# Splitting weight tiles in halves, one of them through the raw ring, and a layer norm's bias placed behind two weight splits

## The chip, the cores and the metric

The kernel runs on one core of a Trainium2 chip. The time is the device time of one execution in microseconds. The kernel before takes 867.73 us, the median of three runs (867.6 to 867.78).

## The reference

One decoder layer over 512 tokens of width 1024, in float32, with inputs and weights in float32:

```
h   = layer_norm(x)                                     # "ln in"
q_g, k_g, v_g, r_g, a, q_lat, kv_lat, gates = split(h @ w_in)
o   = gated_linear_attention(q_g, k_g, v_g, a)          # 4 heads, in chunks; then rms_norm
y_gla = (o * silu(r_g)) @ w_o_gla                       # the GLA output
q, k, v from rms_norm(q_lat) @ w_q_b, rms_norm(kv_lat) @ w_kv_b, with rope
y_mla = softmax_attention(q, k, v) @ w_o_mla            # 8 heads, causal
mix = (sigmoid(gates0) * y_gla + sigmoid(gates1) * y_mla) @ w_out
h   = layer_norm(alpha * h + mix)
out = layer_norm(alpha * h + relu(h @ w_ff1)**2 @ w_ff2)
```

Both kernels compute all of it, with the same products.

## The kernel before, in words

**Float32 by three products.** TensorE multiplies float32 numbers that are rounded to a shorter form (fp32r). Every operand is therefore split into a high part, which ScalarE rounds by a copy, and a low part, which VectorE computes as the rest. A product is three matmuls: high by high, low by high, high by low. For activations the names are h, sh, so, ogT, latT; for weights they are `whi`/`wlo` (or `xh`/`xl` for tiles that stay).

**The stream of weights.** All weight tiles are entries of one list, `stream`, in the order in which the program uses them. `fetch` loads an entry (128 partitions x 1024 float32, 512 KB, or smaller) into a raw buffer `wraw`, a ring of three; `pump` splits entries one or two ahead of use, by one ScalarE copy and one VectorE subtraction over the whole tile, into `whi` and `wlo`, rings of two. Buffers come free in the order of the rings: a raw buffer when its split is done, a `whi` buffer when TensorE has used it for the last time. An entry may have `"fine"` (split per k-row), `"gates"` (instructions behind which its split must stand) and a `"home"`: "r" puts its two parts in two `wraw` buffers instead.

**Seven products instead of eight.** Large products are done as Strassen-like units of seven products with sums of weight tiles and of activations: "11", "t1", "22", "t2", "t3", "21", "t4" (t marks a sum of weights, which lies in a buffer `wq`). The units in the middle of the kernel are `g0` and `g1` (the two halves of the gates) and `yg` (the GLA output). Each product has two column groups (0 and 1) with a weight tile of 4 k-rows x 256 columns each, and a tile serves 24 matmuls of 256 columns (L1299 to L1301).

**Order of use.** `lat` (the latents, two tiles of 2 x 360 columns at a time), q, k, v, r, then `g0` and `g1`, then `yg` 11, t1, 22, t2, then the first rope part of the queries (`qr`, L279 to L281), `yg` t3, then the pair 0 of heads: `qn`, `kn` (L279 to L281) and `mv` (the values, L313 to L315), then `yg` 21. `latT` are latent tiles loaded back from HBM (`latd`) for them, on SyncE's queue like the weights; they use the buffers in which raw weights and sums lay.

**The front.** The first two token tiles are normalised and transposed first, and the latents of these two are computed (`gemm_tm` with the first two `tts`) while `ln_in1` normalises the third and fourth (`x_112`, `x_114` in the rows): statistics (`bst`, `mvin`), the power on GpSimd, the bias `nmr` on VectorE, then the application on ScalarE. Their transposes (L505) follow on TensorE, and `h` on ScalarE from them. The splits of latent weight tiles lie between on ScalarE and VectorE; `issue_after` and `chain` say which instruction must stand behind which.

The order of an engine's instructions is set when the kernel is built: a scheduler arranges the instructions of the program within its dependencies, and an edit at one place can move rows at others. Each engine runs its row of instructions strictly in that order.

Of the kernel before, what the change touches and what calls it, by code (L numbers as in the profile page):

```python
# [19 lines left out]
P = 128  # L20
T = 512
D = 1024
NT = T // P
# [29 lines left out]
def tile_hybrid_block(ctx: ExitStack, tc: tile.TileContext, I, out, dbg=None):  # L53
    nc = tc.nc
# [49 lines left out]
    chain = {}  # L104
# [18 lines left out]
    mm = nc.tensor.matmul  # L123
# [17 lines left out]
    xt = []  # L141
# [12 lines left out]
    ident = ca[:, 0:P]  # L154
# [14 lines left out]
    stream = []  # L169
# [41 lines left out]
    def pump(i):  # L211
        fetch(i + 1 + DMA_AHEAD)
        while st["spl"] < min(len(stream), i + 2 + SPLIT_AHEAD):
            e = stream[st["spl"]]
            if st["spl"] > i + e.get("ahead", SPLIT_AHEAD) and not e["res"]:
                break
            nk, n = e["nk"], e["n"]
            hi, lo = [A([P, nk, T * 2 // nk], F32R, w) for w in HOME["a" if e["res"] else e.get("home", "w")]]
            raw = e["src"]() if "src" in e else e.pop("raw")
            with ExitStack() as gates:  # L220
                for g in e.get("gates") or st["gates"] or (st.get("pt", ()) if e.get("late") else ()):
                    gates.enter_context(tc.issue_after(g.ins))
                for k in [slice(i, i + 1) for i in range(nk)] if e.get("fine") else [slice(0, nk)]:
                    st["ins"] = act(hi[:, k, :n], raw[:, k, :n], AF.Copy)
                    st["lo"] = vtt(lo[:, k, :n], raw[:, k, :n], f(hi[:, k, :n]), op=ALU.subtract)
            st["gates"] = ()
            e["w"] = (hi, lo)
            if "post" in e:
                e["post"](raw)
            if "post2" in e:  # L230
                later[st["spl"] + 2] = lambda p=e["post2"], r=raw: p(r)
            later.pop(st["spl"], lambda: None)()
            st["spl"] += 1
# [57 lines left out]
        tick(width)  # L291
        return accs

    def gemm_tm(pls, xs, n, evac, width=None, tts=range(NT), guard=None, ks=None, accs=None, new=None, fine=False):
        accs = {} if accs is None else accs
        ticks = [0]
        share = n <= 256 and len(pls) == 1 and len(tts) == NT
        nk = pls[0]["nk"]
        for k in ks or range(nk):
            ws = [weights(pl, k) for pl in pls]  # L300
            first, last = k == 0, k == nk - 1
            for tt in tts:
                c = slice(tt * P, (tt + 1) * P)
                xh, xl = xs[k][:, 0, c], xs[k][:, 1, c]
                for j, (hi, lo) in enumerate(ws):
                    if first:
                        if share and tt % 2:
                            accs[tt, j] = accs[tt - 1, j][:, 256:]
                        else:
                            accs[tt, j] = (new or MM)()  # L310
                    o = accs[tt, j][:, :n]
                    opens = first and not (share and tt % 2)
                    mm(o, xh, hi[:, :n], start=opens, stop=False, skip_group_check=share)  # L313
                    mm(o, xh, lo[:, :n], start=False, stop=False, skip_group_check=share)  # L314
                    mm(o, xl, hi[:, :n], start=False, stop=last, skip_group_check=share)  # L315
                ticks[0] += 1
                if fine is True or fine and ticks[0] % fine == 0:
                    tick(width)
            if not last and not fine:
                tick(width)  # L320
        if evac is None:
            return accs
        if guard:
            guard()
        todo = [(tt, j) for tt in tts for j in range(len(pls))]
        for i, (tt, j) in enumerate(todo):
            evac(tt, j, accs[tt, j])
            if i == len(todo) // 2 - 1:
                pump(pls[-1]["idx"][-1] + 1)
        tick(width)  # L330
# [65 lines left out]
    def plan_unit(*seq):  # L396
        for key, op in seq:
            for g in range(UNITS[key][2]):
                PL[key, op, g] = len(stream)
                e = {"nk": 4, "n": 256, "res": False}  # L400
                if op[0] != "t" and (op, key) not in HELD:
                    e["dmas"] = [(slice(0, 4), u_src(key, int(op[0]) - 1, int(op[1]) - 1, g), None)]
                else:
                    e["src"] = lambda q=(key, (op, g)): WQ[q]
                    if key == "g0" and op in ("t1", "t2"):
                        e["ahead"], e["home"] = 2, "wr"[g]
                if op == ("t1" if key == "g0" else "22"):
                    e["post"] = lambda raw, q=(key, "t1", "t2", g): u_sum(*q, WQ[q[0], ("22", q[3])] if q[0] == "g0" else raw)
                    if key == "f1":
                        e["post2"] = lambda raw, q=(key, "12", "t3", g): u_sum(*q, raw)  # L410
                elif op == "21" and key == "yg":
                    e["post"] = lambda raw, g=g: u_sum("yg", "t2", "t4", g, raw)
                elif op == "t2" and key == "g1":
                    e["post"] = lambda raw, g=g: u_acc("g1", "t2", "t4", g, "21")
                elif op == "t2" and key != "yg":
                    e["post2" if key == "f1" else "post"] = lambda raw, q=(key, "t2", "t4", g): u_sum(*q, WQ[q[0], ("21", q[3])])
                stream.append(e)
# [53 lines left out]
        fb += nb  # L471


    def ln_rows(src, dst, mv, on_act=False, behind=None):
        bst = S([P, 2, 6], F32, "bst")
        for j in range(2):
            with ExitStack() as gates:
# [6 lines left out]
        if on_act is not False:  # L484
            nmr = S([P, 1], F32, "nmr")
            chain.pop("dve", None)
            behind = st["nmr"] = stt(nmr, mv[:, 0:1], -1.0, mv[:, 1:2], op0=ALU.mult, op1=ALU.mult)
            for j in range(2):
                c = slice(j * T, (j + 1) * T)
# [8 lines left out]
    def ln_transpose(rows, g, b, outs, hf, alt=False, n="h0"):  # L498
        tk = slice(hf * 256, (hf + 1) * 256)
        for k in range(NK):  # L500
# [1 line left out]
                outs.append(A([P, 2, T], F32R, n) if n == "h0" else (B([P, T], F32R, n), B([P, T], F32R, n)))  # L502
            p = MM() if alt and k in (4, 5) else PX()
            for i in range(2):
                nc.tensor.transpose(p[:, i * P:(i + 1) * P], rows[2 * hf + i][:, k * P:(k + 1) * P],  # L505
                                    identJ if hf and n == "h0" else ident)
            tmp = B([P, 256], F32, "lnt")
            hi, lo = part(outs[k], 0, tk), part(outs[k], 1, tk)
            ha = act(hi, p[:, :256], AF.Identity, scale=g[:, k:k + 1], bias=b[:, k:k + 1])
# [648 lines left out]
    def ln_in1():  # L1158
        for i in range(4):
            yield  # L1160
        for tt in (2, 3):
            chain.update(dve=st["lo"] if tt == 2 else st["nmr"])
            ln_rows(xt[tt], xt[tt], mvin[:, tt, :], on_act=((0, 1), (0,))[tt - 2])
            chain.clear()
            stream[tt + 3]["gates"] = (st["var"],)
            yield
            if tt == 2:
                yield
# [35 lines left out]
    for hf in range(2):  # L1204
# [6 lines left out]
            finish(t_ln1)  # L1211
            st["gates"] = st["h0"]
        for i in range(2):
            gemm_tm([PL["lat", i]], hT, half, ev_lat(i), tts=(2 * hf, 2 * hf + 1), guard=lat_guard if i and not hf else None)
    t_lat = spawn(latents())
    t_he = spawn(h_early())
    gemm_fm(PL["q"], hT, T, ev_q)
# [607 lines left out]
```

## Time and profile before

| | |
|---|---|
| median of three runs | 867.73 us |
| the profiled execution | 867.63 us |
| its span | 865.8 us |
| mean granted clock of TensorE | 0.998 |
| TensorE busy | 853.8 us, 99% |
| VectorE, ScalarE, GpSimd busy | 656.5, 491.9, 136.5 us |
| chain that ended last | TensorE 95%, VectorE 3%, ScalarE 1% |

A row of the timeline gives the start and duration in us from the span's start, the engine, the source line (L111 is the helper through which ScalarE and VectorE instructions are issued), the operation, the names out<-in, the shape, and how many such rows in a run are put together (x2). In square brackets stands how long the engine was idle before it, and what released it. Matmuls overlap: each lasts longer than the distance to the next one's start. A group row gives the count, the busy sum, the mean duration in ns, and the idle time ahead of them. A row by windows gives the window, its length, and for TensorE, its weight load, VectorE, ScalarE and GpSimd the busy us with the number of instructions, then granted clock, share of the DMA engines and GB/s.

### The profile page before, as it was taken

Reading aid. Unit: us, or ns where it says so; the run is one execution under the profiler, and the core shown is the slowest. Engines: PE = TensorE matmul, PEld = TensorE weight load, DVE = VectorE, ACT = ScalarE, POOL = GpSimd, SP = SyncE. Lnnn points to the kernel's source line nnn. Section 1 sums busy time; section 2 is a strip of 40 time slices with the busy share of each in tenths; the row PEclk is TensorE's granted clock in tenths of the full one; section 3 lists DMA queues with packets and bytes.
Section 4 is the critical chain, followed back from the end, with each engine's and each line's share of the span. In section 5 each row is a group of like instructions: output and inputs, shape, how many; then the busy total and the mean of one; then the engine's idle time right before and its main releaser. Section 6 shows DMA issues by size and latency. Waiting matters only on the chain.

```text
span 865.8 us, 13210 instructions
## 1 busy us (share of the span) xinstructions
PE 853.8 (99%) x4887; PEld 752.8 (87%) x4887; DVE 656.5 (76%) x1141; ACT 491.9 (57%) x863; POOL 136.5 (16%) x179
## 2 busy tenths in 40 slices
PE   8999999999999999999999999999999999999996
PEld 7988888889999998988888889988888888889985
DVE  7857889977578858897856878985567546888865
ACT  6556977655566754565745334475466446766820
POOL 1530001110221103030000021005301520141000
PEclk9999999999999999999999999999999999999999
DMA  9896946696649916233155355009922990499312
GB/s 317 226 199 175 345 148 167 212 264 209 148 148 238 205 43 171 56 104 98 32 176 217 120 167 190 1 1 267 256 61 51 304 214 16 104 243 232 106 69 75
DMA packets 101231, 137.94 MB, mean 159 GB/s; under 512 B 13201, under 2 KB 66116, under 8 KB 101168
## 3 DMA queue, kind: packets, MB, share of 16 engines
q1 hardware_dynamic: 76512, 91.35, 33.6%
q0 software_dynamic: 22784, 41.10, 22.7%
q10 hardware_dynamic: 1872, 4.66, 1.4%
q8 instruction: 38, 0.62, 0.3%
q14 instruction: 25, 0.20, 0.1%
HBM read 113.49 MB, written 8.91 MB: 141 GB/s over the span
## 4 chain that ended last, share of the span: by engine, by line
PE 95%; DVE 3%; ACT 1%; DMA 0%; issue 0%; POOL 0%; POOLq 0%; DVEq 0%
PE mm L279 10%; PE mm L280 10%; PE mm L281 10%; PE mm L1301 6%; PE mm L1299 6%; PE mm L1300 6%; PE mm L314 5%; PE mm L315 5%; PE mm L313 5%; PE px L1633 3%; PE px L1634 3%; PE px L1635 3%; PE mm L1633 2%; PE mm L1634 2%; PE mm L1635 2%; PE mm L863 1%
## 5 line engine op out<-in xcount | busy, mean ns | idle before, releaser
L111 DVE TENSOR_TENSOR wlo<-wraw,whi 128x1024 fp32r<-128x1024 f32 (+2 forms) x96 | 96.0, 1006 | 65.2 <-ACT whi L111 65.1
L111 ACT ACTIVATE whi<-wraw 128x1024 fp32r<-128x1024 f32 (+2 forms) x96 | 84.1, 884 | 77.2 <-PE mm L280 20.7
L111 DVE TENSOR_TENSOR wlo<-wq,whi 128x1024 fp32r<-128x1024 f32 x52 | 63.6, 1223 | 31.9 <-ACT whi L111 31.7
L280 PE MATMUL mm<-h,whi 128*128 128x512 f32 x224 | 87.2, 389 | 0.0
L279 PE MATMUL mm<-h,whi 128*128 128x512 f32 x224 | 87.1, 390 | 0.0
L281 PE MATMUL mm<-h,wlo 128*128 128x512 f32 x224 | 83.2, 390 | 0.0
L111 ACT ACTIVATE whi<-wq 128x1024 fp32r<-128x1024 f32 x52 | 55.0, 1058 | 33.6 <-PE mm L1300 16.1
L1652 POOL DMA_DIRECT2D res<-ev x42 | 38.4, 1064 | 180.7 <-ACT ev L111 150.0
L1301 PE MATMUL mm<-sh,wlo 128*128 128x256 f32 x176 | 50.0, 284 | 0.3 <-DVE wlo L111 0.2
L1299 PE MATMUL mm<-sh,whi 128*128 128x256 f32 x176 | 50.0, 284 | 0.0
L1300 PE MATMUL mm<-sh,whi 128*128 128x256 f32 x176 | 49.8, 283 | 0.0
L279 PEld LDWEIGHTS mm<-h,whi 128*128 128x128 f32 x224 | 42.1, 188 | 8.8
L281 PEld LDWEIGHTS mm<-h,wlo 128*128 128x128 f32 x224 | 42.0, 188 | 8.7
L280 PEld LDWEIGHTS mm<-h,whi 128*128 128x128 f32 x224 | 42.1, 188 | 8.6
L111 ACT ACTIVATE relu<-mm 128x512 f32<-128x512 f32 x26 | 15.2, 594 | 41.9 <-PE mm L281 41.9
L111 ACT ACTIVATE xh<-wraw 128x1024 fp32r<-128x1024 f32 (+1 forms) x24 | 24.1, 1014 | 26.1 <-PE mm L315 15.2
L111 DVE TENSOR_TENSOR xl<-wraw,xh 128x1024 fp32r<-128x1024 f32 (+1 forms) x24 | 27.9, 1171 | 11.8 <-ACT xh L111 11.8
L1301 PEld LDWEIGHTS mm<-sh,wlo 128*128 128x128 f32 x176 | 33.8, 192 | 0.7 <-DVE wlo L111 0.7
L1300 PEld LDWEIGHTS mm<-sh,whi 128*128 128x128 f32 x176 | 33.8, 192 | 0.0
L1299 PEld LDWEIGHTS mm<-sh,whi 128*128 128x128 f32 x176 | 33.8, 192 | 0.0
L1301 PE MATMUL mm<-h,wlo 128*128 128x256 f32 x112 | 32.1, 287 | 0.0
L1299 PE MATMUL mm<-h,whi 128*128 128x256 f32 x112 | 31.8, 284 | 0.0
(487 smaller groups left out, 2784.0 us busy)
## 6 DMA issues: line engine op xcount, KB each, us to landing
wraw<-in_w_ff_dram SPq DMA_DIRECT2D x36, 512.0 KB, 5.0
wraw<-in_w_in_dram SPq DMA_DIRECT2D x30, 512.0 KB, 5.1
wq<-in_w_ff_dram POOLq DMA_DIRECT2D x26, 512.0 KB, 9.4
res<-ev POOLq DMA_DIRECT2D x42, 256.0 KB, 9.9
wq<-in_w_in_dram POOLq DMA_DIRECT2D x20, 512.0 KB, 10.1
wq<-in_w_in_dram SPq DMA_DIRECT2D x18, 512.0 KB, 7.5
hsd<-hs SPq DMA_DIRECT2D x16, 256.0 KB, 3.9
xr<-hsd SPq DMA_DIRECT2D x16, 256.0 KB, 4.3
```

The source lines that it names most:

```text
L111: ins = op(*a, **k)
L279: mm(o, hi[:, c], xh, start=first, stop=False)
L280: mm(o, hi[:, c], xl, start=False, stop=False)
L281: mm(o, lo[:, c], xh, start=False, stop=last)
L313: mm(o, xh, hi[:, :n], start=opens, stop=False, skip_group_check=share)
L314: mm(o, xh, lo[:, :n], start=False, stop=False, skip_group_check=share)
L315: mm(o, xl, hi[:, :n], start=False, stop=last, skip_group_check=share)
L1299: mm(oa, hi[:, k, c], xh, start=opens and k == 0 and a == 0, stop=False, skip_group_check=True)
L1300: mm(oa, hi[:, k, c], xl, start=False, stop=False, skip_group_check=True)
L1301: mm(oa, lo[:, k, c], xh, start=False, stop=k == 3, skip_group_check=True)
L1633: mm(o, xh[:, c], hi[:, pp], start=opens, stop=False, skip_group_check=True)
L1634: mm(o, xh[:, c], lo[:, pp], start=False, stop=False, skip_group_check=True)
```

## The change

It has three parts.

1. Every weight tile of `g1` and `yg` gets `"cut": 2`: its split is done in two halves of two k-rows (128 x 512 each), high and low of the first half, then of the second.
2. Column group 1 of `yg` t3 gets the home "r": its two parts lie in two buffers of the raw ring instead of a `whi` and a `wlo` buffer.
3. In the front, while the third token tile is normalised, the splits of stream entries 5 and 6 are placed between its variance and its bias; before, entry 5 stood behind the third tile's variance and 6 behind the fourth's, and now 7 stands behind the fourth's. TensorE's matmuls of the last k-row of the second latent half are put behind the transpose number 1 of the new tokens (`held`, `st["tp"]`).

```diff
@@ pump
-                for k in [slice(i, i + 1) for i in range(nk)] if e.get("fine") else [slice(0, nk)]:
+                step = 1 if e.get("fine") else nk // e.get("cut", 1)
+                for k in [slice(i, i + step) for i in range(0, nk, step)]:
                     st["ins"] = act(hi[:, k, :n], raw[:, k, :n], AF.Copy)
                     st["lo"] = vtt(lo[:, k, :n], raw[:, k, :n], f(hi[:, k, :n]), op=ALU.subtract)
@@ gemm_tm(..., held=False)
-                    mm(o, xh, hi[:, :n], start=opens, stop=False, skip_group_check=share)
+                    with ExitStack() as gates:
+                        if last and held and tt == tts[0]:
+                            gates.enter_context(tc.issue_after(st["tp"].ins))
+                        mm(o, xh, hi[:, :n], start=opens, stop=False, skip_group_check=share)
@@ plan_unit
                 e = {"nk": 4, "n": 256, "res": False}
+                if key in ("g1","yg"):
+                    e["cut"] = 2
+                if (key, op, g) == ("yg", "t3", 1):
+                    e["home"] = "r"
@@ ln_rows(..., between=None)
             chain.pop("dve", None)
+            if between is not None:
+                between()
             behind = st["nmr"] = stt(nmr, mv[:, 0:1], -1.0, mv[:, 1:2], op0=ALU.mult, op1=ALU.mult)
@@ ln_transpose
-                nc.tensor.transpose(p[:, i * P:(i + 1) * P], rows[2 * hf + i][:, k * P:(k + 1) * P],
-                                    identJ if hf and n == "h0" else ident)
+                tp = nc.tensor.transpose(p[:, i * P:(i + 1) * P], rows[2 * hf + i][:, k * P:(k + 1) * P],
+                                         identJ if hf and n == "h0" else ident)
+            if n == "h0" and k == 1:
+                st["tp"] = tp
@@ ln_in1
+        def splits():
+            stream[5]["gates"] = (st["var"],)
+            pump(4)
+            chain.update(dve=st["lo"])
+
         for tt in (2, 3):
             chain.update(dve=st["lo"] if tt == 2 else st["nmr"])
-            ln_rows(xt[tt], xt[tt], mvin[:, tt, :], on_act=((0, 1), (0,))[tt - 2])
+            ln_rows(xt[tt], xt[tt], mvin[:, tt, :], on_act=((0, 1), (0,))[tt - 2], between=splits if tt == 2 else None)
             chain.clear()
-            stream[tt + 3]["gates"] = (st["var"],)
+            if tt == 3:
+                stream[7]["gates"] = (st["var"],)
@@ the latents' calls of gemm_tm
+                    held=i and not hf)
```

How the rows move at the places of which the prediction speaks. First VectorE in the front, before; `nmr_289` and `nmr_315` are the biases of the third and fourth token tile, `xl` low parts of latent weight tiles:

```order
L111 TENSOR_TENSOR xl_300<-wlo_233,xh_299 128x2x360
L111 SCALAR_TENSOR_TENSOR nmr_289<-mvin 128x1
L111 BN_STATS bst_309<-x_114 128x6 x2
L111 BN_AGGR mvin<-bst_309 128x2
L111 TENSOR_SCALAR mvin<-mvin 128x1
L111 TENSOR_TENSOR xl_328<-wlo_235,xh_327 128x2x360
L111 SCALAR_TENSOR_TENSOR nmr_315<-mvin 128x1
L111 TENSOR_SCALAR x_114<-x_114,mvin 128x512
L111 TENSOR_TENSOR xl_369<-wraw_237,xh_368 128x2x360
```

The same place now:

```order
L111 TENSOR_TENSOR xl_291<-wlo_233,xh_290 128x2x360
L111 TENSOR_TENSOR xl_295<-wlo_235,xh_294 128x2x360
L111 SCALAR_TENSOR_TENSOR nmr_289<-mvin 128x1
L111 BN_STATS bst_313<-x_114 128x6 x2
L111 BN_AGGR mvin<-bst_313 128x2
L111 TENSOR_SCALAR mvin<-mvin 128x1
L111 TENSOR_TENSOR xl_369<-wraw_237,xh_368 128x2x360
L111 SCALAR_TENSOR_TENSOR nmr_319<-mvin 128x1
L111 TENSOR_SCALAR x_114<-x_114,mvin 128x512
```

Both low parts stand ahead of the first bias now, and the third one ahead of the second bias. TensorE behind the fourth token tile's last early transpose, up to the first matmul on the new h (`h_16_140` with `mm_459`), before:

```order
L505 MATMUL px_378<-ca,x_114 128x128
L314 MATMUL mm_340<-xl_369,h_41_202 128x360
L315 MATMUL mm_340<-xh_368,h_41_202 128x360
L314 MATMUL mm_344<-xl_369,h_41_202 128x360
L315 MATMUL mm_344<-xh_368,h_41_202 128x360
L313 MATMUL mm_340<-xh_368,h_44_210 128x360
L314 MATMUL mm_340<-xl_369,h_44_210 128x360
L315 MATMUL mm_340<-xh_368,h_44_210 128x360
L313 MATMUL mm_344<-xh_368,h_44_210 128x360
L314 MATMUL mm_344<-xl_369,h_44_210 128x360
L315 MATMUL mm_344<-xh_368,h_44_210 128x360
L313 MATMUL mm_459<-xh_136,h_16_140 128x360
```

And now (the same source lines are five lines further down):

```order
L516 MATMUL px_378<-ca,x_114 128x128
L318 MATMUL mm_340<-xh_368,h_44_210 128x360
L319 MATMUL mm_340<-xl_369,h_44_210 128x360
L320 MATMUL mm_340<-xh_368,h_44_210 128x360
L318 MATMUL mm_459<-xh_136,h_16_140 128x360
```

Ten matmuls stood between, three are left; seven have moved ahead of the transposes. SyncE at `yg` t3, where it loads weights of qn (`w_q_b`), of kn (`w_kv_b`) and two latent tiles, before:

```order
L208 DMA wraw_3784<-in_w_q_b_dram 128x2x128
L208 DMA wraw_3857<-in_w_q_b_dram 128x2x128 x2
L208 DMA wraw_3895<-in_w_kv_b_dram 128x2x128 x2
L1414 DMA latT_3661<-latd_1180 128x1024
L1414 DMA latT_3663<-latd_1220 128x1024
```

And now:

```order
L208 DMA wraw_3830<-in_w_q_b_dram 128x2x128
L1435 DMA latT_3703<-latd_1180 128x1024
L1435 DMA latT_3705<-latd_1220 128x1024
L208 DMA wraw_3905<-in_w_q_b_dram 128x2x128 x2
L208 DMA wraw_3943<-in_w_kv_b_dram 128x2x128 x2
```

The loads of qn's second tile and of kn's tile have gone behind the latents; by the ring, the first takes the buffer of qn's first tile and the second that in which t3's high part lay. ScalarE at the same place, with the splits of qr's second tile (`whi_3758`) and of t3's groups 0 and 1 (`whi_3768`, `whi_3786`), before:

```order
L111 ACTIVATE whi_3758<-wraw_3701 128x2x256
L111 ACTIVATE u_688_3734<-mm_3500 128x512
L111 ACTIVATE tabw_3741<-cs 128x512
L111 ACTIVATE tabw_3749<-sn 128x512
L111 ACTIVATE tab_3739<-px_3740 128x512
L111 ACTIVATE whi_3768<-wq_3377 128x1024
L111 ACTIVATE whi_3786<-wq_3380 128x1024
```

And now:

```order
L111 ACTIVATE wraw_3832<-wq_3406 128x512 x2
L111 ACTIVATE whi_3802<-wraw_3745 128x2x256
L111 ACTIVATE u_688_3778<-mm_3532 128x512
L111 ACTIVATE tabw_3785<-cs 128x512
L111 ACTIVATE tabw_3793<-sn 128x512
L111 ACTIVATE tab_3783<-px_3784 128x512
L111 ACTIVATE whi_3812<-wq_3403 128x512 x2
```

Group 1 (`wraw_3832`) has moved from the last place to the first, ahead of qr's second tile; each split counts two rows now.

More of the change, by code (lines that the diff above doesn't have):

```diff
@@ L292, in gemm_fm, with gemm_tm @@
         return accs
[L294 removed]
+    def gemm_tm(pls, xs, n, evac, width=None, tts=range(NT), guard=None, ks=None, accs=None, new=None, fine=False,
+                held=False):
         accs = {} if accs is None else accs
@@ L471, in tile_hybrid_block, with ln_rows @@
         fb += nb
-    def ln_rows(src, dst, mv, on_act=False, behind=None):
+    def ln_rows(src, dst, mv, on_act=False, behind=None, between=None):
         bst = S([P, 2, 6], F32, "bst")
@@ L1213, in tile_hybrid_block @@
         for i in range(2):
-            gemm_tm([PL["lat", i]], hT, half, ev_lat(i), tts=(2 * hf, 2 * hf + 1), guard=lat_guard if i and not hf else None)
+            gemm_tm([PL["lat", i]], hT, half, ev_lat(i), tts=(2 * hf, 2 * hf + 1), guard=lat_guard if i and not hf else None,
+                    held=i and not hf)
     t_lat = spawn(latents())
```

## The prediction

> **What bounds the kernel now.** I read the page's totals and chain first, then the waits of TensorE (us in total, times, longest), of which four belong to places that the change touches.
>
> ```profile
> span 865.8 us, 13210 instructions
> ...
> PE 95%; DVE 3%; ACT 1%; DMA 0%; issue 0%; POOL 0%; POOLq 0%; DVEq 0%
> ...
> PE mm L314 <- DVE xl L111: 0.4, 1, 0.4
> PE mm L314 <- DVE wlo L111: 0.2, 1, 0.2
> PE mm L1299 <- ACT whi L111: 0.2, 1, 0.2
> PE mm L1301 <- DVE wlo L111: 0.2, 1, 0.2
> ```
>
> TensorE is the bound: 95% of the chain, and the change leaves its 4718 rows of work as many as they are. So the time can only move by TensorE's idle moments, and the waits listed make 1.0 us. They understate a stall: matmuls overlap, and their ends are modelled. I therefore read starts against the usual spacing, in TensorE's timeline (start, us, instruction):
>
> ```profile
> 23.80 0.60 PE L505 MATMUL px<-ca,x 128*128 128x128 f32 x4
> 24.78 0.43 PE L314 MATMUL mm<-xl,h 128*128 128x360 f32 x1 [0.38 <-DVE xl L111]
> ...
> 28.75 0.32 PE L315 MATMUL mm<-xh,h 128*128 128x360 f32 x1
> 28.91 0.32 PE L313 MATMUL mm<-xh,h 128*128 128x360 f32 x1
> ...
> 275.78 0.28 PE L1299 MATMUL mm<-sh,whi 128*128 128x256 f32 x1
> 275.90 0.28 PE L1300 MATMUL mm<-sh,whi 128*128 128x256 f32 x1
> 276.33 0.39 PE L1301 MATMUL mm<-sh,wlo 128*128 128x256 f32 x1 [0.15 <-DVE wlo L111]
> 276.55 0.28 PE L1299 MATMUL mm<-sh,whi 128*128 128x256 f32 x1
> ...
> 279.19 0.28 PE L1300 MATMUL mm<-sh,whi 128*128 128x256 f32 x1
> 279.60 0.39 PE L1301 MATMUL mm<-sh,wlo 128*128 128x256 f32 x1
> ...
> 296.85 0.28 PE L1300 MATMUL mm<-ogT,whi 128*128 128x256 f32 x1
> 297.13 0.39 PE L1301 MATMUL mm<-ogT,wlo 128*128 128x256 f32 x1
> ...
> 325.63 0.28 PE L1300 MATMUL mm<-ogT,whi 128*128 128x256 f32 x1
> 326.15 0.39 PE L1299 MATMUL mm<-ogT,whi 128*128 128x256 f32 x1 [0.24 <-ACT whi L111]
> ...
> 332.23 0.39 PE L281 MATMUL mm<-latT,wlo 128*128 128x512 f32 x1
> 332.58 0.50 PE L279 MATMUL mm<-latT,whi 128*128 128x512 f32 x1
> ...
> 338.83 0.40 PE L313 MATMUL mm<-whi,latT 128*128 128x256 f32 x2
> 339.47 0.39 PE L314 MATMUL mm<-wlo,latT 128*128 128x256 f32 x1 [0.25 <-DVE wlo L111]
> ```
>
> A 256-wide matmul starts 0.12 us after the last (275.78, 275.90), a 360-wide one 0.16, a 512-wide one 0.23 (the 332 rows' usual step). After a stall the next step is longer too: 276.33 to 276.55 is 0.22, so each stall has 0.1 us of refill behind it. That gives what each costs: at 24 us four transposes end near 24.1 and the next matmul starts at 24.78, 0.6 + 0.1 = 0.7; at 276, 0.43 - 0.12 + 0.1 = 0.4; at 279, 0.4; at 297, 0.28 - 0.12 + 0.1 = 0.25; at 326, 0.52 - 0.12 + 0.1 = 0.5; at 332.6, 0.35 - 0.23 + 0.1 = 0.2; at 339, 0.64 - 0.24 + 0.1 = 0.5. **The sum, 2.95 us, is the ceiling of what the change can win.**
>
> **Part one, halves (second gate unit and GLA output).** It adds instructions and moves no arithmetic. Groups by shape (busy us, mean ns of one), the low parts concerned, and VectorE's load in its fullest stretch (after the sum, mean busy columns PE, PEld, DVE, ACT, POOL):
>
> ```profile
> L111 DVE TENSOR_TENSOR wlo<-wraw,whi 128x1024 fp32r<-128x1024 f32 x60 | 73.5, 1224 | 52.5 <-ACT whi L111 52.4
> L111 DVE TENSOR_TENSOR wlo<-wraw,whi 128x512 fp32r<-128x512 f32 x30 | 20.0, 686 | 11.3 <-ACT whi L111 11.3
> L111 ACT ACTIVATE whi<-wraw 128x1024 fp32r<-128x1024 f32 x60 | 63.5, 1058 | 42.6 <-PE mm L280 14.8 <-PE mm L1300 7.4 <-DMA wraw<-in_w_ff_dram 6.7
> L111 ACT ACTIVATE whi<-wraw 128x512 fp32r<-128x512 f32 x30 | 18.1, 628 | 25.4 <-issue 12.5 <-PE mm L280 5.3 <-PE mm L1300 5.1
> ...
> 275.05 1.22 DVE L111 TENSOR_TENSOR wlo<-wraw,whi 128x1024 fp32r<-128x1024 f32 x1
> 278.33 1.22 DVE L111 TENSOR_TENSOR wlo<-wq,whi 128x1024 fp32r<-128x1024 f32 x1
> ...
> 280.00:300.00 20.00, 20.00 (x167) 19.80 (x167) 18.74 (x32) 15.36 (x30) 3.69 (x3) 1.00 0.95 216
> ```
>
> A tile's first low half is there 1.22 - 0.69 = 0.53 us earlier than the whole, and where ScalarE leads, another 1.06 - 0.63 = 0.43. At 276 the half ends at 275.05 + 0.69 = 275.74, before the 276.02 at which TensorE wants it: 0.4 saved. At 279 it ends at 279.02 against 279.31 wanted, but TensorE comes 0.4 earlier by then, and VectorE's queue is what is late: 0.15 to 0.4 saved. At 297, 0 to 0.25 for the same reason. I take **-0.85**, bounds -0.4 (only the first) and -1.05.
>
> The price: 28 tiles (two units, seven products, two column groups) get one more instruction on each of two engines, at most 2 x 0.686 - 1.224 = 0.15 us on VectorE and 2 x 0.628 - 1.058 = 0.2 on ScalarE. Back to back they overlap, the lower end is near 0. Seven such tiles lie in 280 to 300, so VectorE goes from 18.74 to at most 19.8 of 20: still covered by TensorE's work, without slack. If that cover is gone, each further 0.1 on VectorE is 0.1 of time.
>
> [...]
>
> **Part two, the GLA output's third sum in the raw ring.** The sum's high and low part take two turns of a ring of three, so, as SyncE's rows in the change's section show, qn's second tile and kn's tile are now loaded behind two latent tiles. On ScalarE the sum's split of group 1 comes forward ahead of qr's second tile. It no longer needs a whi buffer that TensorE frees, so 326's 0.5 goes; and mv's low part now stands ahead of gate products on VectorE, so 339's 0.5 can go. SyncE's and ScalarE's rows of before, with median us to landing:
>
> ```profile
> 321.49 0.88 SPq L208 DMA_DIRECT2D wraw<-in_w_kv_b_dram  x2
> 326.02 1.70 SPq L1414 DMA_DIRECT2D latT<-latd  x2
> ...
> wraw<-in_w_kv_b_dram SPq DMA_DIRECT2D x16, 128.0 KB, 2.3
> latT<-latd SPq DMA_DIRECT2D x5, 512.0 KB, 4.1
> latd<-latT SPq DMA_DIRECT2D x5, 512.0 KB, 6.0
> ```
>
> The row at 326.02 is released by the low part of the sum's group 0, whose place on VectorE hardly moves. So the latents still go out at 326.0 to 327.7, then qn's two loads to 328.6. Alone they land by 328.15 + 2.3 = 330.5; behind the second latent, whose 4.1 runs from 326.9 to 331.0, somewhat later: 330.5 to 331.5, split 0.63 later, 331.1 to 332.1. TensorE wants them at 332.35 - 0.5 = 331.85. That is between 0.2 won (332.6's stall) and 0.25 lost. Kn's load now waits for the sum's last matmul, near 331.2, and its second piece lands at 331.2 + 0.45 + 2.3 = 334.0; split 334.6, low part 335.3, wanted 334.6 (twelve 512-wide steps after 331.85) and 335.1: 0 to 0.3 lost. Before, that load went out at 321.49. Queued behind it on SyncE are mv's load and the 512 KB of the GLA output's next product; mv's is not wanted before 337.4, so they have 2 us to spare. Part two: **-0.7**, between -1.2 and, if 339's wait stays and both loads are late, 0.05 lost.
>
> **Part three, the front.** On VectorE the bias (nmr) of the third token tile now follows two low parts (xl) of weights instead of one:
>
> ```profile
> 20.75 0.91 DVE L111 TENSOR_TENSOR xl<-wlo,xh 128x720 fp32r<-128x720 f32 x1
> 22.11 0.16 DVE L111 SCALAR_TENSOR_TENSOR nmr<-mvin 128x1 f32<-128x1 f32 x1 [0.44 <-POOL mvin L483]
> 23.82 0.91 DVE L111 TENSOR_TENSOR xl<-wlo,xh 128x720 fp32r<-128x720 f32 x1
> 27.18 1.93 ACT L111 ACTIVATE h<-px,ca 128x256 fp32r<-128x256 f32 x4
> ```
>
> The second low part moves from 23.82 to 20.75 + 0.9 = 21.6 and is done at 22.5, long before 24.1: 0.7 goes. What is late next is the bias, 22.11 to 22.5, and with it the third tile's normalisation on ScalarE (behind it there: the fourth tile's, a weight split and the quarters of h) and the fourth tile's statistics, each by 0.4. The gate on `st["tp"]` and the later bias also change TensorE's order: the third tile's transposes move behind the first matmuls of the last weight tile, seven more matmuls (0.16 each) precede the fourth tile's, and three instead of ten stand between those and the first use of the new h. That use was at 28.91, 1.2 us after h's first quarter was ready, at 27.18 + 1.93 / 4 = 27.7. Now the quarter comes 0.4 later by the bias and 0.3 later by a copy of lat put ahead of it on ScalarE, near 28.4, and is wanted seven matmuls earlier than before (1.15) but for what else moves, some 28.2: 0.2 + 0.1 lost, perhaps 0.1 more at the next transposes. Net **-0.3**, between -0.7 (h in time) and +0.3 (ScalarE's copies queue, 1.0 lost).
>
> **Sum:** -0.85 - 0.7 - 0.3 = -1.85 against the profiled execution (its span 865.8, itself 867.63, within 0.1 of the median 867.73): **865.9 us**. What can be told from no change is 0.2%, 1.74 us: faster means below 866.0, so the forecast stands on the line.
>
> **Rivals.** (a) *The stalls only move*: VectorE full by the halves, h late, qn late: -0.4 + 0.05 + 0.0 = -0.35, **867.4**. For it: 18.74 of 20. Against: TensorE's wants come only every 2.9 us per tile (24 x 0.12). (b) *Slower: the ring's loads stand behind the latents.* If qn's second load (out at 328.15) and kn's (out at 331.65) take the 6.0 us of the 512 KB stores instead of 2.3, they land at 334.15 and 337.65, split 334.8 and 338.3. TensorE wants the first at 331.85: 2.95 lost; the second at 334.8 + 2.75 = 337.55: 0.75 lost. Against 0.85 + 0.3 + 1.0 won: +1.55, **869.3**. It decides where the two landings cost over 2.15 together, from some 5.1 us each. For it: the loads leave a ring that had four us of lead. Against: 2.3 is the median of sixteen such loads, some of them beside the latents. (c) *All goes*: no new stall, close to the ceiling: -2.8, **864.9**. Against: h's three matmuls of cover. (d) *It does not do what it says*: TensorE's reordered rows find other late operands at the same places, one for one: **867.7**. For it: 2.95 us of stalls are only seven places of 0.2 to 0.7 us.
>
> **How the numbers follow.** Forecast 0.48 (faster 0.28, same 0.2), its own range 865.2 to 866.6; (a) 0.19, same; (b) 0.12, slower 0.07, same 0.05; (c) 0.17, faster; (d) 0.04, same 0.02, slower 0.02. Faster 0.45, same 0.46, slower 0.09. The range runs from 864.7 (the ceiling) to 868.0; above it lies most of (b).
>
> **What would show it.** Right: no wait on xl near 24 us, none on wlo between 275 and 298, none on whi near 326; a wait of some 0.2 us on h near 28. Wrong: qn's or kn's whi waiting for a DMA, and TensorE for it, over 1 us at 332 to 336; VectorE at 20 of 20 in 280 to 300; new waits where nothing was moved on purpose.

## The result

The changed kernel takes **865.85 us** (median of 15 runs, 865.31 to 867.21) against 867.73 before (15 runs, 867.27 to 868.1): 1.88 us less, a ratio of 0.998 with a 95% interval of 0.9973 to 0.9988. The interval lies wholly below 1, so the change is faster. Its median is 0.22% lower, just past the 0.2% (866.0) at which the prediction drew its line, and the interval reaches to both sides of that line. The forecast was missed by 0.05 us. The runs below show that this nearness is largely luck: two terms were larger than predicted, one smaller, and one loss stood where none was expected.

The profiled execution took 866.70 us, the second longest of the 15. Its page and TensorE's waits:

```profile
span 864.9 us, 13264 instructions
...
PE 97%; DMA 1%; ACT 1%; DVE 1%; issue 0%; POOLq 0%; POOL 0%; DVEq 0%; SPq 0%; ACTq 0%
...
PE wake L167 <- DVE still L164: 1.5, 1, 1.5
PE mm L318 <- ACT whi L111: 1.5, 1, 1.5
PE px L516 <- ACT x L111: 0.8, 1, 0.8
PE mm L280 <- ACT PT L111: 0.6, 1, 0.6
PE px L516 <- DVE x L111: 0.4, 1, 0.4
PE mm L280 <- ACT h L111: 0.3, 1, 0.3
```

All four waits that the prediction quoted are gone: no row for xl, wlo, or L1320 on whi is left. In their place stands one that was not there before, 1.5 us of L318 on `whi`, the longest wait behind the start. The prediction had put a wait of over 1 us at 332 to 336 among its signs of being wrong, though for qn's or kn's tile. TensorE's timeline of the changed kernel shows the places:

```profile
27.55 0.60 PE L516 MATMUL px<-ca,x 128*128 128x128 f32 x4
27.90 0.41 PE L318 MATMUL mm<-xh,h 128*128 128x360 f32 x1
28.15 0.33 PE L319 MATMUL mm<-xl,h 128*128 128x360 f32 x1
28.31 0.33 PE L320 MATMUL mm<-xh,h 128*128 128x360 f32 x1
28.73 0.43 PE L318 MATMUL mm<-xh,h 128*128 128x360 f32 x1
29.00 0.33 PE L319 MATMUL mm<-xl,h 128*128 128x360 f32 x1
...
275.82 0.28 PE L1320 MATMUL mm<-sh,whi 128*128 128x256 f32 x1
275.94 0.28 PE L1321 MATMUL mm<-sh,whi 128*128 128x256 f32 x1
276.06 0.28 PE L1322 MATMUL mm<-sh,wlo 128*128 128x256 f32 x1
276.18 0.28 PE L1320 MATMUL mm<-sh,whi 128*128 128x256 f32 x1
...
334.59 0.40 PE L280 MATMUL px<-latT,whi 128*128 128x512 f32 x1
334.82 0.39 PE L281 MATMUL px<-latT,whi 128*128 128x512 f32 x1
336.67 0.51 PE L318 MATMUL mm<-whi,latT 128*128 128x256 f32 x2 [1.46 <-ACT whi L111]
```

At 28.31 the next start is 0.42 later instead of 0.16, and the one behind it 0.27: 0.36 us of wait on the new h. Near 276 the starts are 0.12 apart without a gap. At 334.82 the next start comes 1.85 us later instead of 0.23: with the refill behind it (336.67 to 337.01, 0.34 for two steps of 0.12), **1.7 us lost** ahead of the first matmul of mv, the tile of the values' weights. SyncE and ScalarE say why that operand was late; their rows at the place:

```profile
322.32 2.77 SPq L1435 DMA_DIRECT2D latT<-latd  x2
325.20 0.90 SPq L208 DMA_DIRECT2D wraw<-in_w_q_b_dram  x2
330.08 1.91 SPq L208 DMA_DIRECT2D wraw<-in_w_kv_b_dram  x4
332.15 2.83 SPq L208 DMA_DIRECT2D wraw<-in_w_o_gla_dram  x2
...
329.42 0.63 ACT L111 ACTIVATE whi<-wraw 128x512 fp32r<-128x512 f32 x1 [2.01 <-PE mm L1321]
333.23 0.63 ACT L111 ACTIVATE whi<-wraw 128x512 fp32r<-128x512 f32 x1 [1.53 <-DMA wraw<-in_w_kv_b_dram]
335.98 0.63 ACT L111 ACTIVATE whi<-wraw 128x512 fp32r<-128x512 f32 x1 [1.64 <-DMA wraw<-in_w_kv_b_dram]
```

The four loads x4 are kn's and mv's, and they go out at 330.08, when the sum's last matmuls set the ring's buffers free. The three splits are qn's second tile, kn and mv. Qn and kn are in time; mv's split waits for its load until 335.98, 4.0 us after the last of the four went out (330.08 + 1.91 = 331.99); that last one landed at 335.88. TensorE's row had asked for the tile at 335.05 (334.82 + 0.23). The rows, as the kernel issues them there, `px` kn and `mm` mv:

```order
L280 MATMUL px_3987<-latT_3703,whi_3959 128x512
L281 MATMUL px_3987<-latT_3703,whi_3959 128x512
L280 MATMUL px_3988<-latT_3703,whi_3959 128x512
L281 MATMUL px_3988<-latT_3703,whi_3959 128x512
L318 MATMUL mm_4016<-whi_3980,latT_3703 128x256
L318 MATMUL mm_4023<-whi_3980,latT_3703 128x256
L282 MATMUL px_3987<-latT_3703,wlo_3960 128x512
L282 MATMUL px_3988<-latT_3703,wlo_3960 128x512
```

Before, both L313 rows of mv stood behind all of kn's. Now two of mv's matmuls stand ahead of kn's last eight.

VectorE's and ScalarE's busy time rose by 1.3 and 2.6 us, to 657.8 and 494.5. In the fullest stretch VectorE went from 18.74 to 19.03 (third busy column), and two halves take 1.29 us where one whole took 1.22:

```profile
280.00:300.00 20.00, 20.00 (x169) 20.00 (x168) 19.03 (x39) 15.80 (x35) 3.52 (x3) 1.00 0.96 228
...
274.74 1.29 DVE L111 TENSOR_TENSOR wlo<-wraw,whi 128x512 fp32r<-128x512 f32 x2
```

So a second half costs 0.07 us, not the 0.15 of two durations (2 x 686 against 1224 ns). The next instruction's start says the same: it comes 1.20 us after the pair's start here (275.94) and 1.14 after the whole's before (275.05, 276.19). So back to back about half of what two durations would add does not show.

### The profile page after: what moved, and what is told of

Read it like the earlier page. It is cut to its first block, busy times and chain, and to the rows that moved or that the text cites. A ratio compares the mean times of both kernels' runs of the same rounds, so it can differ in the third digit from the quotient of the medians.

```text
span 864.9 us, 13264 instructions
## 1 busy us (share of the span) xinstructions
PE 852.7 (99%) x4887; PEld 752.6 (87%) x4887; DVE 657.8 (76%) x1169; ACT 494.5 (57%) x891; POOL 136.0 (16%) x179
## 4 chain that ended last, share of the span: by engine, by line
PE 97%; DMA 1%; ACT 1%; DVE 1%; issue 0%; POOLq 0%; POOL 0%; DVEq 0%; SPq 0%; ACTq 0%
PE mm L280 10%; PE mm L281 10%; PE mm L282 10%; PE mm L1322 6%; PE mm L1320 6%; PE mm L1321 6%; PE mm L320 5%; PE mm L318 5%; PE mm L319 5%; PE px L1654 3%; PE px L1656 3%; PE px L1655 3%; PE mm L1654 2%; PE mm L1656 2%; PE mm L1655 2%; PE mm L876 1%
## 5 line engine op out<-in xcount | busy, mean ns | idle before, releaser
L111 DVE TENSOR_TENSOR wlo<-wq,whi 128x1024 fp32r<-128x1024 f32 (+1 forms) x66 | 63.6, 980 | 28.1 <-ACT whi L111 28.1
L111 ACT ACTIVATE whi<-wq 128x1024 fp32r<-128x1024 f32 (+1 forms) x66 | 55.3, 860 | 32.0 <-PE mm L1321 15.3
L1320 PE MATMUL mm<-sh,whi 128*128 128x256 f32 x176 | 49.9, 284 | 0.0
L1320 PEld LDWEIGHTS mm<-sh,whi 128*128 128x128 f32 x176 | 33.8, 192 | 0.0
L1320 PE MATMUL mm<-h,whi 128*128 128x256 f32 x112 | 31.8, 284 | 0.0
```

Source lines behind the costliest of these rows:

```text
L111: ins = op(*a, **k)
L1320: mm(oa, hi[:, k, c], xh, start=opens and k == 0 and a == 0, stop=False, skip_group_check=True)
```

## How the stalls were summed

For each profiled run I added up, over TensorE's matmuls, the distance from one start to the next less a fixed step: 0.118 us for 256 columns, 0.164 for 360, 0.228 for 512, close to the medians of before (0.120, 0.164, 0.227), and for 128 columns 0.07, which was assumed (the median of before is 0.109). The places are counted from the first 360-wide matmul on, because the start itself varies: that matmul begins between 10.05 and 10.71 us in the profiles, whatever the kernel, with a wait on x that some have and others don't. The step of 0.07 is too short for the front's transposes, whose starts lie 0.11 apart (four from 23.80 to 24.13 in the kernel before). So each figure of the front's column holds about 1 us that is no stall, the same in every kernel, and only the differences between rows count. Two stretches are clean and agree to 0.06 us between kernels that have the same part: 12 to 60 us behind that matmul (the front) and 255 to 305 (second gate unit and the GLA output's first products). In the stretch of the sum and the first pair of heads, 305 to 335, small gaps come and go by some 0.4, so there single waits are read.

| kernel | front, 12 to 60 | gates, 255 to 305 | median us, less before's of the same batch |
|---|---|---|---|
| before | 1.84 | 1.87 | |
| the change | 1.70 | 0.83 | -1.88 |
| e1, halves alone | 1.89 | 0.83 | -1.57 |
| e2, ring alone | 1.90 | 1.87 | -1.44 |
| e3, front alone | 1.69 | 1.87 | -0.15 |
| e4, halves and front | 1.69 | 0.83 | -1.67 |
| e6, halves and ring | 1.89 | 0.83 | -1.99 |
| e8, the change, mv last | 1.70 | 0.83 | -2.48 |
| e9, e8 without the hold in front | 2.14 | 0.83 | -1.81 |

The gates' column separates the kernels with the halves (0.83) from those without (1.87) in every profile. The medians are less sharp: the ratios' intervals are 0.0015 to 0.0021 wide, 1.3 to 1.8 us, so a difference of a few tenths between two rows counts only where two kernels ran side by side and their runs barely overlap.

## The experiments

**The parts one by one.** e1 leaves out the ring and the front, e2 the halves and the front, e3 the halves and the ring (shortened; where the front is left out, its gates and order are as before):

```diff
 # e1                                        # e2                               # e3
-if (key, op, g) == ("yg", "t3", 1):         -if key in ("g1","yg"):            -if key in ("g1","yg"):
-    e["home"] = "r"                         -    e["cut"] = 2                  -    e["cut"] = 2
-between=splits, held=...                    -between=splits, held=...          -if (key, op, g) == ("yg", "t3", 1):
                                                                                -    e["home"] = "r"
```

> Only the halves (part one); no raw ring for the sum, front as before. Theory A (halves take the stalls on late weight parts): TensorE's stalls at 276, 279 and 297 us go, 1.07 us by the rows of before, and at 326 the first half of the sum's high part is 0.43 us earlier, so most of that 0.5 goes too: 866.2 to 866.7, 1.1 to 1.6 us less than before. The stalls at 24, 332.6 and 339 us stay. Rival B (VectorE full, the stalls move one tile on): within 0.4 us of before, 867.3 to 867.7.

Measured: 866.21 (865.93 to 868.11) against 867.78, ratio 0.9983 (0.9974 to 0.9992). Theory A, at the end of its range: 1.57 us less, with only 1.04 of it in the gates' stretch. The rest is at the sum: there the first half of its high part is early enough without the ring, so the halves alone take 326's stall too. 332.6's is gone too, and 339's has become one of the next product's first matmul (L1311) on its own `whi`, 0.55 us with its refill. It stands there because in this kernel's row that matmul comes right behind the first two of mv:

```profile
337.32 0.40 PE L318 MATMUL mm<-whi,latT 128*128 128x256 f32 x2
338.01 0.39 PE L1311 MATMUL mm<-ogT,whi 128*128 128x256 f32 x1 [0.29 <-ACT whi L111]
```

> Only the sum in the raw ring (part two), whole tiles, front as before. Theory A (the ring takes the stalls at 326 and 332.6 us, 0.7 us, and gives back a wait of TensorE on the first mv tile near 335 us, 1.7 us in the one profiled run of the changed kernel, less in most): 867 to 868.5, a wider spread than before's, and in the profile a wait on whi ahead of L318's or L313's first matmul on latT. Rival B (the mv wait belongs to another part): 866.8 to 867.1, no such wait.

Measured: 866.34 (866.14 to 867.22), ratio 0.9984 (0.9975 to 0.9992). **Theory A fell**: 1.44 us less, no wait on mv at all. In this kernel mv's rows stand behind kn's on TensorE, as before: its split starts at 335.51 and TensorE asks for it at 338.21, where the change asks at 335.05.

```profile
335.51 0.62 ACT L111 ACTIVATE whi<-wraw 128x512 fp32r<-128x512 f32 x1
...
338.21 0.40 PE L318 MATMUL mm<-whi,latT 128*128 128x256 f32 x2
```

Here the split waits for its turn on ScalarE and not for the load, which landed at 333.10. So the wait on mv is not the ring's alone; two of mv's matmuls stand ahead of kn's last in the kernels that have the whole ring and the halves together (the change, e6), and in none that lacks one of them (e1, e2, e4, e5). Why the scheduler places them so is open. Even 866.8 to 867.1, rival B's figure, was too little: the ring takes all of 326, 332.6 and 339.

> Only the front (part three). Theory A (0.7 us of stall on xl at 24 us goes, 0.36 comes back as a wait on the new h near 28.5 us): 867.4, 0.35 us less than before. Rival B (no wait on h when the rest is as before, or other rows late): 867.0 with all of it won, or 867.7 and over with none.

Measured: 867.63 (867.28 to 868.7), ratio 0.9999 (0.9991 to 1.0008): no difference that can be told, 0.15 less in the median, which agrees with the 0.15 fewer us of stalls in the front's stretch. The stall at 24 us is gone, 0.7, and most of it is back:

```profile
28.40 0.33 PE L320 MATMUL mm<-xh,h 128*128 128x360 f32 x1
28.82 0.43 PE L318 MATMUL mm<-xh,h 128*128 128x360 f32 x1
29.09 0.33 PE L319 MATMUL mm<-xl,h 128*128 128x360 f32 x1
```

0.36 on the new h, as theory A has it, and the rest in small gaps. The mechanism is theory A's; of its 0.35 us less than half is left.

**The parts in pairs.** e4 is e1 with the front, e6 the change without it (the edits against the change, shortened).

```diff
 # e4                                        # e6
-if (key, op, g) == ("yg", "t3", 1):         -between=splits if tt == 2 else None
-    e["home"] = "r"                         -held=i and not hf
```

> The change without its second part: halves and front only. Theory A (the parts add, the ring's own gain of 0.7 us and its mv wait of about 0.9 us nearly cancel): 865.8 to 866.3, as fast as the whole change, and a spread of some 0.5 us over the runs instead of 1.9. Rival B (the ring is what the change lives on): 866.6 or more.

Measured: 866.11 (865.56 to 867.63), ratio 0.9977 (0.9968 to 0.9986): Theory A for the median. Its spread was 2.1 us, not 0.5; ten of eleven runs lie within 0.7, and the eleventh is the profiled one, in which the next product's first matmul loses 1.1 us (0.98 and the refill), twice what it loses in e1: its load took 6.0 us to land instead of e1's 5.1. Against the change's 1.88 e4 wins 1.67: with the halves in place, the ring is worth only some 0.2 us (0.4 between e1 and e6), less than medians of different batches can tell. Both aim at the same stalls, and the ring brings the wait on mv.

> The change without its third part: halves and ring, front as before. Theory A: 0.35 us more than the change, 866.2, with the stall of 0.7 us at 24 us back and no wait on h near 28.5. Rival B (the front's gain is eaten by other rows): 865.8.

Measured: 865.87 (865.58 to 867.32), ratio 0.9981 (0.9972 to 0.999), 1.99 us less than before, no more than the change. Rival B by the median, though the stall at 24 us is back in its trace and the front's sum stands at 1.89. In the same batch ran e7, whose rows turned out to be the change's (below), with the same median of 865.87. So what the front is worth shows in the traces and not in the time: 0.15 is under what these medians can tell.

**The wait on mv.** e5 puts only the sum's high part into the ring, so that kn is loaded before the sum ends and only mv waits for it; e8 leaves the loads as they are and moves TensorE's request (shortened):

```diff
 # e5
-                    e["home"] = "r"
+                    e["home"] = "m"           # HOME["m"] = ("wraw", "wlo")
 # e8, in gemm_fm and gemm_tm; st["mv"] is set around the first pair's mv
-                mm(o, lo[:, c], xh, start=False, stop=last)
+                st["fm"] = mm(o, lo[:, c], xh, start=False, stop=last)
+                        if first and st.get("mv"):
+                            gates.enter_context(tc.issue_after(st["fm"].ins))
```

> The change, with only the sum's high part in the raw ring and its low part in a wlo buffer. The ring then turns once less: the first kn tile is loaded before the sum ends, and only the first mv tile waits for it. In TensorE's row the first two matmuls of mv stand behind all of kn's, 1.8 us later than in the change. Theory A (the late mv load is what the change still loses): mv's wait goes, median 864.7 to 865.2, 0.7 to 1.2 us under the change, spread under 0.8 us. Rival B (the mv wait in the profiled run was a rare one, the median holds none): 865.7 to 866.0, as the change.

Measured: 865.79 (865.36 to 866.12), ratio 0.9976 (0.9967 to 0.9985), 2.07 us less than before: rival B's figure, but not for rival B's reason. The wait on mv is gone and the spread is 0.8, but another has come in its place: the next product's first matmul loses 0.55 us, as in e1.

> The change, with mv's first matmuls held behind kn's last one on TensorE (eight 512-wide matmuls, 1.8 us, later than in the change); nothing else moves, SyncE's queue is the same. Theory A (TensorE's row asks for mv 1.8 us too early): the wait near 335 us falls by 1.8 us to about nothing, median 864.8 to 865.3, spread under 0.8 us. Rival B (whatever delays mv's load delays kn's low part or the next tile as well): 865.7 to 866.

Measured: **865.38** (865.08 to 865.97) against 867.86, ratio 0.9974 (0.9964 to 0.9984). Theory A. The other rows are as in the change (on TensorE a matmul near 344 changes places too); the load goes out as there, mv's split starts as late (335.68), and TensorE no longer minds; no gap of over 0.1 us is left at the place:

```profile
336.63 0.39 PE L282 MATMUL px<-latT,wlo 128*128 128x512 f32 x1
336.85 0.40 PE L320 MATMUL mm<-whi,latT 128*128 128x256 f32 x2
337.09 0.39 PE L321 MATMUL mm<-wlo,latT 128*128 128x256 f32 x1
...
335.68 0.63 ACT L111 ACTIVATE whi<-wraw 128x512 fp32r<-128x512 f32 x1 [1.43 <-DMA wraw<-in_w_kv_b_dram]
```

Beside e7 in its own batch, that is 0.49 us less. The change itself and e8's kernel then ran once more, together.

> The change itself once more, for comparison with the next two on one chip: 865.85, 1.9 us under before, a spread of over 1 us, and a wait on mv's whi of 0.5 to 1.7 us in the profile.

> The kernel of e8 (the change with mv's first matmuls behind kn's last) once more, beside the change on one chip. Theory A (mv's wait costs the change's median some 0.5 us): 865.4, 0.4 to 0.6 us under the change. Rival B (the difference between the two in separate batches was the batch's): within 0.15 us of the change.

Measured: the change 865.40 (865.0 to 865.77), e8's kernel **864.94** (864.68 to 865.23), before 867.26; ratios 0.9978 (0.9969 to 0.9987) and 0.9972 (0.9962 to 0.9983). Theory A. All eight runs of e8's kernel lie under the change's median; the change's own spread was 0.8 us this time. The wait on mv costs the median 0.46 us; in the profile of this batch it was 0.5 with its refill, in that of the first 1.7.

**Why mv's load is late.** It goes out at the end of the sum, and right behind it go two loads of 512 KB for the next product. e7 and e10 were to move these away (e10 shortened):

```diff
 # e7, in fetch, ahead of the next product's first load
+            if st["dma"] - 1 == PL.get(("yg", "21", 0)):
+                A([P, 1, T], F32, "wraw")
 # e10, in fetch, for both loads of the next product; fetch is called again behind each split
+            if st["dma"] == PL.get(("yg", "21", 0)) and st["spl"] < st["dma"]:
+                return
+            if "yg21" in st and st["dma"] - 1 in st["yg21"]:
+                with tc.issue_after(st["lo"].ins):
+                    nc.vector.memset(raw[:, 0, :2], 0.0)
```

> The change, with one turn of the raw ring left unused ahead of the next product's first tile, so that its two loads of 512 KB go out behind kn's and mv's splits instead of right behind mv's load. Theory A (these loads share the DMA engines with mv's and hold up its last pieces): mv lands within 2.5 us of its issue, the wait near 335 us falls from 1.7 to under 0.5 us; but the next product's tile can then be late near 341 us, by up to 1 us. Rival B (mv's load is late by its own issue, behind the sum's last matmul and kn's load): the wait stays over 1.2 us.

Measured: 865.87 (864.99 to 866.81), ratio 0.9978 (0.9969 to 0.9986). The edit did nothing: the two loads went out from 332.25, right behind mv's, as in the change (332.15). The rows on TensorE, VectorE, SyncE and GpSimd are the change's, one by one. So the run tells nothing on the question, but is a second sample of the change: its wait on mv was 0.8 us.

> The change, with the two loads of 512 KB for the GLA output's next product held behind the split of the first mv tile (a store of two elements on VectorE into each buffer, ordered behind that split). Theory A (those loads, issued right behind mv's, hold up its last pieces on the DMA engines): mv's split starts near 334.3 instead of 335 to 336, the wait ahead of the first mv matmul falls to under 0.3 us; the next product is then late by up to 3 us near 341. Rival B (mv's load is late by its issue behind the sum's last matmul alone): its split stays at 335 or later, and the wait over 0.8 us.

Measured: 865.52 (865.18 to 867.7), ratio 0.9982 (0.9974 to 0.9991). Here the loads did move, to 335.93 and 337.01:

```profile
329.68 1.91 SPq L213 DMA_DIRECT2D wraw<-in_w_kv_b_dram  x4
335.93 0.37 SPq L213 DMA_DIRECT2D wraw<-in_w_o_gla_dram  x1
...
334.48 0.63 ACT L111 ACTIVATE whi<-wraw 128x512 fp32r<-128x512 f32 x1 [0.65 <-DMA wraw<-in_w_kv_b_dram]
...
334.39 0.39 PE L287 MATMUL px<-latT,whi 128*128 128x512 f32 x1
335.16 0.51 PE L324 MATMUL mm<-whi,latT 128*128 128x256 f32 x2 [0.38 <-ACT whi L111]
```

Mv's split still starts 2.9 us after its last load went out (329.68 + 1.91 = 331.59, 334.48), and 0.65 us are lost (0.77 - 0.23 + 0.1). In the change beside it (e11), with the two loads right behind, the split started 2.8 us after, and 0.5 were lost. Neither theory has its figures: the split starts near theory A's 334.3, the loss lies between the two. But against e11 nothing was won by taking the loads away. By these two profiles about half a us of loss needs no load behind mv's; it comes from the late issue and the early request. The median doesn't settle it, because the next product now pays: the second of its two tiles is late, and TensorE loses 0.34 us on its high and 0.38 on its low part near 345.

In other profiles mv's load took longer, and there the loads right behind can't be the whole reason either. From its issue to its landing, the last of the four took 3.1 to 3.4 us in e6, e7 and e11 and 4.0 to 4.8 in the change, e8, e9 and e12, all with those two loads behind, and 3.3 in e10 without. In e8, e9 and e12 the whole neighbourhood was late: mv's other load, issued 0.5 us earlier, took 3.9 to 4.3 us (2.4 to 2.9 in the other five), and GpSimd's three transfers (`QS<-q`) issued beside it 4.1 to 4.6 (2.8 to 3.9 in the others). A list of the DMA packets shows one thing that only these three profiles have at that moment: a packet of the queue for instructions, 16 KB, that took 0.9 to 1.4 us and began between 332.3 and 333.1. In e10 it came at 334.6, behind mv's landing, and in the change, e6, e7 and e11 at 336.3 or later. That points at this packet for the three, but no run moved it, so it is not shown. The change's first profile has it at 338.7 and yet lost most, because the last of the four loads alone landed late. What makes that load long in some executions and not in others **stays open**.

**The hold in the front.** e9 is e8's kernel without the hold on the last matmuls (against e8's, shortened):

```diff
-                    held=i and not hf)
```

> The kernel of e8 without the change's hold on TensorE's last matmuls in the front; the splits stay ahead of the bias. In TensorE's row no matmul is left between the fourth token tile's transposes and the first use of the new h (three in the change, ten before). Theory A (what the front wins at 24 us comes back as a wait on the new h, which the later bias makes late, and the hold only shortens it): the wait near 28.5 us grows from 0.36 to 0.8 or more, median 865.8 to 866.1. Rival B (the hold itself makes the transposes late): the wait goes, median 865.0 to 865.1.

Measured: 865.45 (864.97 to 865.86), ratio 0.9978 (0.9969 to 0.9987), 0.5 us slower than e8's kernel in the same batch. Theory A; the front's stalls rise from 1.69 to 2.14. Its profile also loses 0.5 us at mv's low part, because mv's load landed 4.8 us after its issue, the longest of all, and the split started at 336.50:

```profile
27.73 0.60 PE L518 MATMUL px<-ca,x 128*128 128x128 f32 x4
28.91 0.43 PE L320 MATMUL mm<-xh,h 128*128 128x360 f32 x1 [0.58 <-ACT h L111]
29.18 0.32 PE L321 MATMUL mm<-xl,h 128*128 128x360 f32 x1
```

The last transpose starts near 28.06, and with nothing left between, the new h is waited for 0.8 us. So the two edits of the front belong together: with the splits ahead of the bias alone, the front's stalls are larger than before the change (2.14 against 1.84).

## Why the prediction was right, and where it wasn't

*What bounds it, and the reading of stalls by starts.* Right. Every stall that the prediction named is gone in the change, and the sums by starts agree with the medians: the gates' -1.04 and the sum's place make e1's -1.57, and the front's -0.14 is of the size of e3's -0.15, which alone can't be told from nothing. TensorE's instructions number 4887 in both profiles; the 4718 of the prediction stands in neither.

*Part one, -0.85.* Right in kind, undersized: -1.04. The step that failed is "VectorE's queue is what is late" at 279 and 297, for which 0.15 to 0.4 and 0 to 0.25 were allowed; both went whole. VectorE's queue itself moved forward. The first halves of ScalarE's splits release it earlier: 0.39 us at a low part that waits for ScalarE (270.85, before 271.24), of which 0.31 are left at the tile for 276 (274.74, before 275.05) and 0.25 at the tile for 279 (278.08, before 278.33). The two rows of before, 0.98 us idle and none:

```profile
271.24 1.23 DVE L111 TENSOR_TENSOR wlo<-wraw,whi 128x1024 fp32r<-128x1024 f32 x1 [0.98 <-ACT whi L111]
...
278.33 1.22 DVE L111 TENSOR_TENSOR wlo<-wq,whi 128x1024 fp32r<-128x1024 f32 x1
```

And the latter now:

```profile
278.08 1.29 DVE L111 TENSOR_TENSOR wlo<-wq,whi 128x512 fp32r<-128x512 f32 x2
```

The prediction had that lead in its terms ("where ScalarE leads, another 0.43") and did not carry it along the queue. It also did not have that the halves reach the sum at 326, so that parts one and two are not to be added. Apart they win 1.57 and 1.44, with the front 3.16 together, and the change wins 1.88.

*The price of the halves.* Right: covered. VectorE paid 0.07 us a tile, the middle of the predicted 0 to 0.15. Its busy time rose by 1.3 us over 28 tiles, where 28 times the upper end of that would be 4.2.

*Part two, -0.7.* The three stalls went, 1.2 us, with e2's 1.44 a little more. Two steps were wrong. The latents were to go out at 326.0 still, released by the low part of the sum's group 0, "whose place on VectorE hardly moves". But the first now waits for group 1's low part, which moved to the front:

```profile
320.97 1.28 DVE L111 TENSOR_TENSOR wraw<-wq,wraw 128x512 fp32r<-128x512 f32 x2
323.44 1.29 DVE L111 TENSOR_TENSOR wlo<-wq,whi 128x512 fp32r<-128x512 f32 x2
```

It ends at 322.25, and that of group 0 at 324.73, 1.2 us earlier than before. The latents went out at 322.3 and 324.8, which brought qn's load out at 325.2 to 326.1 instead of 328.6 and left it no trouble at all; kn's was in time as well. And of the loads queued behind kn's, mv's was given "2 us to spare", wanted "not before 337.4". That step read mv's place in the kernel before; in the changed row two of its matmuls stand eight earlier, 1.8 us, and TensorE arrives earlier by what it no longer waits. It asked at 335.05 and lost 0.5 us in the median. The row that uses an operand is as much part of a load's deadline as the row that issues it.

*Part three, -0.3.* Right in mechanism, oversized: -0.14. The stall of 0.7 went, the wait on the new h came back with 0.36 (0.3 was worked out), and small gaps beside it with another 0.2.

*The sum.* -1.04 in the gates, -1.2 to -1.4 at the sum, -0.14 in front, +0.5 at mv: about -2.0, measured -1.88. The forecast of -1.85 came out by luck: two undersized gains stand against a loss that was not foreseen and an oversized gain.

*The rivals.* (a) did not happen: VectorE reached 19.03 of 20. (b) was right that loads of the ring could come late, with the wrong tile, the wrong reason and eight times the price in the median (3.7 against 0.46): it had qn's and kn's loads take 6.0 us behind the latents; they took 2.2 to 3.4, and mv's was late, issued at the end of the sum for an early request. (c), the change without a new loss, is nearly e8's kernel: 2.3 to 2.5 us under before where (c) had 2.8.

## What to carry to other kernels

Where one engine is the bound and is 99% busy, read its gaps from start to start: the waits listed made 1.0 us, the stalls 2.95, and e8's kernel won 2.3 to 2.5 of them. When a change reorders rows, take the deadline of each load from the new row of the engine that uses it, not from the old trace; two matmuls put ahead cost here a quarter of the gain, and holding them back gave it back. Two edits that aim at one stall are not added: halves and ring won 1.57 and 1.44 us alone, and 1.99 together.

## What the runs showed that was not expected

Two instructions of half the size back to back take 1.29 us on VectorE where one takes 1.22, though alone they last 0.69 each: two durations show twice what splitting cost this full queue. And a load of 128 KB, 2.3 us to landing in the median of sixteen before, took 3.1 to 4.8 us at one place in eight profiles of nearly the same kernel.
